# Four of sixteen transposes of the residual stream, moved from the last product into the out projection

## The chip, the core and the metric

The kernel runs on one core of a Trainium2 chip. The metric is the device time of one execution in microseconds (us). A profile is one execution recorded instruction by instruction; its span runs from the first to the last instruction and is a little shorter than the device time.

## The reference

One layer of a decoder with two attention mixers, batch 1, 256 tokens, width 1024, all in float32:

```python
h = rmsnorm(x, norm1_g)
proj = h @ w_in                      # queries, keys, values, gates
y_nsa  = nsa_attention(...)          # 8 heads, three branches
y_moba = moba_attention(...)         # 8 heads
mixed = g_nsa * (y_nsa @ w_up_nsa) + g_moba * (y_moba @ w_up_moba)
x = x + mixed @ w_out                # the out projection; this sum is x1 below
h2 = rmsnorm(x, norm2_g)
u = relu(h2 @ w_ff1)                 # 1024 -> 4096
x = x + (u * u) @ w_ff2              # 4096 -> 1024, the last product
return rmsnorm(x, norm_f_g)
```

## The kernel before

**Chunks and slots.** All weights come from memory in chunks of 128 partitions by up to 2048 numbers (1 MB), listed in `CHUNKS` in the order of use. Chunk c is loaded into a `raw` tile by SyncE (L71), split by ScalarE into a rounded high part `whi` (L87) and by VectorE into the rest `wlo` (L89), and used by TensorE. Each of the three tiles has three buffers. A product of float32 numbers is done as three matmuls: high by high, high by low, low by high (`mm3`; every one of them is recorded at the helper's line L187). The matmuls of one chunk make a slot. While slot c runs, chunk c+2 is split and chunk c+5 is loaded.

**Order inside a slot.** `run_slot` takes the list of the slot's matmuls and the events registered by `at(pos, f, ...)`. It sorts the events by `pos` and issues each of them ahead of the matmul whose place in the list, as a share of its length, reaches `pos`; so `at(0.5, ...)` in a slot of 48 matmuls comes after the first 24. Issue order is the order of every engine's own program: the schedule is written out by hand, and no planner reorders it.

**Transposed stream.** Up to the last product everything is kept with the model dimension on the partitions: `xT` (part of the tile `gx`) holds the input so, eight blocks of 128 by 256. The out projection has four slots (`for i in range(4)`, L678), each with 2 blocks of 128 model columns. Its matmuls (8 per block, three each, 48 a slot) go to `acc` tiles, and `wout_evac(i)`, issued at 0.02 of the following slot (for the last slot's first block already at 0.52 of that slot), adds the result into `x1T` (the same memory as `xT`; VectorE, L663), scales it by the second norm's gain into `h2h` (ScalarE, L666) and takes the rest `h2l` (VectorE, L669). In the slot i == 1 the attention tiles are given up and the tiles of the last stage opened in their room (`open_ff`), and near its end ScalarE issues the broadcast load of the final gain `gfb` (L687).

**The two products after it.** `ff1` has 16 slots with h2 as moving operand. `ff2` (L801) turns to token rows on the partitions: 16 chunks, each with 24 matmuls of 512 columns into four accumulators `o`, and each chunk is one slot but for the last two, which share one. The rows form of the residual, `FB["x1"]` (named x in the profile), is needed for the row norm `rstd2` in the slot i == 3 and for the last addition in `final_a`.

**The transposes.** `x1_rows` makes that form: for each pair of blocks (k2 = 0 to 3) four transposes of 128 by 128 on TensorE (L719) into one PSUM tile and one copy on ScalarE (L721) into 256 columns of `x1`. The PSUM tiles are three `acc` buffers and `yb`, the single tile that carries attention outputs before and one accumulator of the very last slot after. In the kernel before, all 16 transposes and four copies are issued at 0.5 of the slot i == 1 of `ff2`:

```python
tiles = [acc_tile(), acc_tile(), acc_tile(), ps_y.tile([128, 512], F32, name="yb")]
```

Of the kernel before, what the change touches and what calls it, by code (L numbers as in the profile page):

```python
# [8 lines left out]
F32 = mybir.dt.float32  # L9
F32R = mybir.dt.float32r  # L10
AF = mybir.ActivationFunctionType
# [29 lines left out]
def hybrid_layer(ctx: ExitStack, tc: tile.TileContext, gxd, w, w1c, small, const, gf, out):  # L41
    nc = tc.nc
    act, dve, pool, pe = nc.scalar, nc.vector, nc.gpsimd, nc.tensor
# [5 lines left out]
    ps_y = ctx.enter_context(tc.tile_pool(name="ps_y", bufs=1, space=PS))  # L49
# [6 lines left out]
    def acc_tile():  # L56
        return ps_acc.tile([128, 512], F32, name="acc")
# [35 lines left out]
    ident = cp.tile([128, 128], F32, name="ident")  # L93
# [56 lines left out]
    for k2 in range(4):  # L150
        v = xT[:, 2 * k2:2 * k2 + 2, :]
# [17 lines left out]
    def at(pos, f, *a):  # L169
        ev.append((pos, f, a))  # L170

    def run_slot(mms):
        n = len(mms)
        es = sorted(ev, key=lambda e: e[0])
        ev.clear()
        j = 0
        for i, m in enumerate(mms):
            while j < len(es) and es[j][0] <= i / n:
                es[j][1](*es[j][2])
                j += 1  # L180
            m()
        while j < len(es):
            es[j][1](*es[j][2])
            j += 1
# [24 lines left out]
    def wstat(o, c, off, nk, ncol, ah, al, ks=None, first=0, last=None):  # L209

        r = []
        last = nk - 1 if last is None else last
        for k in (range(nk) if ks is None else ks):
            a = k * ncol + off
            r += mm3(o, hi[c][:, a:a + 128], lo[c][:, a:a + 128], ah[:, k, :], al[:, k, :],
                     k == first, k == last)
        return r

    def split_events(c, hs, ls):
        for i in range(2):  # L220
            at(hs[i], split, c + 2, i, 2, "h")
        for i in range(2):
            if ls[i] <= 1:
                at(ls[i], split, c + 2, i, 2, "l")
        if ls[1] <= 1:
            at(max(ls) + 0.05, load, c + 5)

    def std_events(c):
        split_events(c, (0.0, 0.45), (0.3, 0.46))
# [394 lines left out]
    def two_blocks(c, ah, al, late=8):  # L624

        if late < 8:
            outs = [acc_tile()[:, 0:256] for _ in range(2)]
            whole = None
            order = [range(late), range(late, 8)]
        else:  # L630
            whole = acc_tile()
            outs = [whole[:, 0:256], whole[:, 256:512]]
            order = [range(8)]
        mms = []
        for ks in order:
            for m in range(2):
                mms += wstat(outs[m], c, m * 128, 8, 256, ah, al, ks=ks, last=7)
        return mms, outs, whole


    x1T = xT
    FB = {}
# [30 lines left out]
    def lo_late(pos, c):  # L673
        for k in range(2):
            at(pos, split, c + 2, k, 2, "l")
        at(pos + 0.01, load, c + 5)

    for i in range(4):  # L678
        c = C_WOUT + i
        if i == 0:  # L680
            lo_late(0.03, c - 1)
        split_events(c, (0.0, 0.1), ((0.5, 0.5), (0.3, 0.3), (0.3, 0.3), (9, 9))[i])
        for f, a in prev:
            at(0.02, f, *a)
        if i == 1:
            at(0.01, open_ff)
            at(0.9, lambda: act.dma_start(FB["gfb"], gf[None, :].to_broadcast([128, 1024])))  # L687
        if i == 3:
            outs = [acc_tile()[:, 0:256] for _ in range(2)]
            at(0.52, wout_evac, i, outs, (0,))  # L690
            run_slot([m for j in range(2)
                      for m in wstat(outs[j], c, j * 128, 8, 256, mxh, mxl)])
            prev = [(wout_evac, (i, outs, (1,)))]
        else:
            mms, outs, _ = two_blocks(c, mxh, mxl, 6 if i == 0 else 8)
            run_slot(mms)
            prev = [(wout_evac, (i, outs))]


    def ff1_evac(i, outs, whole):  # L700
# [8 lines left out]
        dve.tensor_tensor(rf, rf, rf, op=ALU.mult)  # L709
        act.activation(h, rf, AF.Copy)  # L710
        dve.tensor_tensor(l, rf, h.bitcast(F32), op=ALU.subtract)

    def x1_rows():
        tiles = [acc_tile(), acc_tile(), acc_tile(), ps_y.tile([128, 512], F32, name="yb")]
        for k2 in range(4):
            v = tiles[k2].rearrange("p (t d) -> p t d", t=2)
            for t in range(2):
                for m in range(2):
                    pe.transpose(v[:, t, m * 128:(m + 1) * 128],  # L719
                                 x1T[:, 2 * k2 + m, t * 128:(t + 1) * 128], ident)  # L720
            act.activation(FB["x1"][:, :, k2 * 256:(k2 + 1) * 256], v, AF.Copy)  # L721

    def rstd2():
        fst = FB["fst"]
# [25 lines left out]
    fst, x1, scr = FB["fst"], FB["x1"], FB["scr"]  # L750
# [3 lines left out]
    def ff2_mms(i, p):  # L754
        c = C_FF2 + i
        t, c0, n = p
        r = []
        for k in range(2):
            kt = 2 * i + k
            lh, ll = (FB[a][:, kt, t * 128:(t + 1) * 128] for a in ("sqh", "sql"))  # L760
            a = k * 1024 + c0
            r += mm3(ops[p][:, 0:n], lh, ll, hi[c][:, a:a + n], lo[c][:, a:a + n],
                     kt == (28 if p == LAST[1] else 0),
                     kt == (27 if p == PARTS[1][1] else 31))
        return r
# [35 lines left out]
    for i in range(15):  # L801
        std_events(C_FF2 + i)
        for f, a in prev:
            at(0.02, f, *a)
        prev = []
        if i == 1:
            at(0.5, x1_rows)
        if i == 3:
            at(0.1, rstd2)
        if i < 14:  # L810
            run_slot([m for p in order for m in ff2_mms(i, p)])
        else:
            ops[LAST[1]] = ps_y.tile([128, 512], F32, name="yb")
            at(0.05, first_part)
            at(0.23, final_a, PARTS[0][0], 0)
            at(0.43, final_a, PARTS[0][1], 1)
            at(0.46, final_b, 0)
            at(0.64, final_a, PARTS[1][0], 0)
            at(0.83, final_a, LAST[0], 1)
            run_slot([m for p in PARTS[0] + PARTS[1][:1] + LAST for m in ff2_mms(14, p) + ff2_mms(15, p)])  # L820
# [85 lines left out]
```

## Time and profile before

| | us |
|---|---|
| median of 3 runs | 395.99 |
| the three runs | 395.70, 395.99, 398.17 |
| device time of the profiled execution | 396.34 |
| its span | 394.5 |
| busy in it: TensorE matmul, weight load | 384.6, 346.3 |
| busy in it: VectorE, ScalarE, GpSimd | 267.5, 204.6, 9.0 |
| mean granted TensorE clock in it | 0.990 of full speed |

PE stands for TensorE's matmuls, PEld for its weight loads, DVE for VectorE, ACT for ScalarE, POOL for GpSimd and SP for SyncE. A letter q behind an engine's name is its instruction queue. A row of the timeline has start, duration, engine, line, operation and operands, and in square brackets how long the engine had been idle and what it waited for. Operand names of a matmul stand as output, then moving operand, then the operand loaded as weights. Rows of the chain view have start, length and what ran. The recorded duration of a matmul is longer than the distance to the next one, since matmuls follow one another in a pipeline; costs on TensorE are therefore read from starts.

### The profile page before, as it was taken

What the parts mean: (1) busy time and instruction counts of PE and PEld (TensorE: products, weight loads), DVE (VectorE), ACT (ScalarE), POOL (GpSimd) and SP (SyncE); (2) the same over time, 40 slices, a digit from 0 to 9 for tenths busy, and PEclk for the clock granted to TensorE, in tenths of its full rate; (3) what the DMA queues carried; (4) which work ended last, traced back from release to release, by engine and by line L of the source; (5) the groups of instructions that cost most, each with busy time, mean ns of one, the idle gap of its engine ahead of it and who ended that gap; (6) DMA issues with size and microseconds to landing.
All of it is one profiled execution on the core that took longest, in us unless ns stands there. A gap on an engine that the chain in (4) does not pass through costs nothing.

```text
span 394.5 us, 6611 instructions
## 1 busy us (share of the span) xinstructions
PE 384.6 (97%) x2687; PEld 346.3 (88%) x2687; DVE 267.5 (68%) x468; ACT 204.6 (52%) x366; POOL 9.0 (2%) x16
## 2 busy tenths in 40 slices
PE   7999999999999999999999999999999999999993
PEld 5888887778988999999999999999998888888883
DVE  5988589798778788867866665666566443444444
ACT  6474546667645555644464556455655563334412
POOL 4300000000000000000000000000000000000001
PEclk8799999999999999999999999999999999999999
DMA  7885623523323343263482655455544637555003
GB/s 240 313 339 214 213 106 114 207 89 126 108 108 107 124 157 149 108 214 106 171 311 96 226 214 185 154 197 213 185 154 195 213 130 268 169 184 208 1 2 106
DMA packets 11694, 66.34 MB, mean 168 GB/s; under 512 B 1296, under 2 KB 3600, under 8 KB 4368
## 3 DMA queue, kind: packets, MB, share of 16 engines
q1 hardware_dynamic: 11232, 65.14, 45.8%
q10 hardware_dynamic: 432, 0.79, 0.5%
q8 instruction: 21, 0.34, 0.3%
q14 instruction: 9, 0.07, 0.1%
HBM read 64.87 MB, written 1.05 MB: 167 GB/s over the span
## 4 chain that ended last, share of the span: by engine, by line
PE 93%; issue 2%; DMA 1%; DVE 1%; ACT 1%; SPq 0%; POOL 0%; POOLq 0%; DVEq 0%
PE acc L187 62%; PE o L187 21%; PE yb L187 3%; PE S L187 2%; PE tp L450 2%; PE tp L187 1%; DMA gx<-in_gx_dram 1%; PE tp L263 1%; DVE wlo L89 0%; PE acc L719 0%; POOL rstd L164 0%; PE tp L387 0%; SPq L71 0%; SPq L114 0%; DVE x L772 0%
## 5 line engine op out<-in xcount | busy, mean ns | idle before, releaser
L89 DVE TENSOR_TENSOR wlo<-raw,whi 128x1024 fp32r<-128x1024 f32 (+2 forms) x128 | 144.4, 1159 | 41.6 <-ACT whi L87 41.5
L87 ACT ACTIVATE whi<-raw 128x1024 fp32r<-128x1024 f32 (+2 forms) x128 | 124.1, 990 | 92.2 <-issue 35.5
L187 PE MATMUL acc<-h2h,whi 128*128 128x256 f32 x256 | 71.9, 281 | 0.0
L187 PE MATMUL acc<-h2l,whi 128*128 128x256 f32 x256 | 71.9, 281 | 0.0
L187 PE MATMUL acc<-h2h,wlo 128*128 128x256 f32 x256 | 71.9, 281 | 0.0
L187 PE MATMUL o<-whi,sqh 128*128 128x512 f32 (+1 forms) x128 | 49.5, 386 | 0.0
L187 PE MATMUL o<-whi,sql 128*128 128x512 f32 (+1 forms) x128 | 49.4, 386 | 0.0
L187 PE MATMUL o<-wlo,sqh 128*128 128x512 f32 (+1 forms) x128 | 49.4, 386 | 0.0
L187 PEld LDWEIGHTS acc<-h2h,whi 128*128 128x128 f32 x256 | 49.2, 192 | 0.0
L187 PEld LDWEIGHTS acc<-h2l,whi 128*128 128x128 f32 x256 | 48.0, 188 | 0.0
L187 PEld LDWEIGHTS acc<-h2h,wlo 128*128 128x128 f32 x256 | 48.0, 188 | 0.0
L187 PE MATMUL acc<-wlo,hTh 128*128 128x512 f32 (+2 forms) x96 | 38.7, 403 | 2.0 <-DVE wlo L89 1.8
L187 PE MATMUL acc<-whi,hTh 128*128 128x512 f32 (+2 forms) x96 | 38.1, 397 | 0.1
L187 PE MATMUL acc<-whi,hTl 128*128 128x512 f32 (+2 forms) x96 | 37.8, 394 | 0.0
L187 PE MATMUL acc<-hTh,whi 128*128 128x256 f32 x128 | 37.6, 293 | 0.0
L187 PE MATMUL acc<-hTl,whi 128*128 128x256 f32 x128 | 36.9, 289 | 0.0
L187 PE MATMUL acc<-hTh,wlo 128*128 128x256 f32 x128 | 36.2, 282 | 0.0
L187 PEld LDWEIGHTS o<-wlo,sqh 128*128 128x128 f32 x128 | 24.0, 188 | 4.9
L187 PEld LDWEIGHTS o<-whi,sql 128*128 128x128 f32 x128 | 24.0, 188 | 4.9
L187 PEld LDWEIGHTS o<-whi,sqh 128*128 128x128 f32 x128 | 24.0, 188 | 4.7
L187 PEld LDWEIGHTS acc<-hTh,whi 128*128 128x128 f32 x128 | 24.3, 190 | 1.4 <-issue 1.4
L187 PEld LDWEIGHTS acc<-hTl,whi 128*128 128x128 f32 x128 | 24.3, 190 | 1.0
(216 smaller groups left out, 613.5 us busy)
## 6 DMA issues: line engine op xcount, KB each, us to landing
raw<-in_ff_dram SPq DMA_DIRECT2D x32, 1024.0 KB, 4.8
raw<-in_gm_dram SPq DMA_DIRECT2D x8, 1024.0 KB, 4.8
raw<-in_wout_dram SPq DMA_DIRECT2D x4, 1024.0 KB, 4.9
raw<-in_q_dram SPq DMA_DIRECT2D x2, 1024.0 KB, 5.6
raw<-in_qm_dram SPq DMA_DIRECT2D x2, 1024.0 KB, 5.3
raw<-in_km_dram SPq DMA_DIRECT2D x2, 1024.0 KB, 4.9
raw<-in_vm_dram SPq DMA_DIRECT2D x2, 1024.0 KB, 4.8
raw<-in_upn_dram SPq DMA_DIRECT2D x2, 1024.0 KB, 4.7
```

The costliest lines, as they stand in the source:

```text
L87: act.activation(hi[c][:, a:b], raw[c][:, a:b], AF.Copy)
L89: dve.tensor_tensor(lo[c][:, a:b], raw[c][:, a:b], hi[c][:, a:b].bitcast(F32), op=ALU.subtract)
L187: pe.matmul(o, l, r, start=start, stop=stop, skip_group_check=True)
L263: pe.transpose(tp[:, j * 256 + t * 128:j * 256 + t * 128 + 128], src[:, t, (2 * i + j) * 128:(2 * i + j + 1) * 128], ident)
L450: pe.transpose(tp[:, dst:dst + 128], P[:, j, src:src + 128], ident)
```

## The change

`x1_rows` is defined earlier and takes a list of block pairs and of PSUM tiles. The pair k2 = 0 (four transposes and one copy) is issued at 0.5 of the slot i == 1 of the out projection and uses `yb`; the other three pairs stay at 0.5 of the slot i == 1 of `ff2` and use three `acc` buffers. The number of instructions and the values that they compute stay what they were.

```diff
+    def x1_rows(k2s, tiles):
+        for k2, tp in zip(k2s, tiles):
+            v = tp.rearrange("p (t d) -> p t d", t=2)
+            for t in range(2):
+                for m in range(2):
+                    pe.transpose(v[:, t, m * 128:(m + 1) * 128],
+                                 x1T[:, 2 * k2 + m, t * 128:(t + 1) * 128], ident)
+            act.activation(FB["x1"][:, :, k2 * 256:(k2 + 1) * 256], v, AF.Copy)
+
     for i in range(4):
         c = C_WOUT + i
...
         if i == 1:
             at(0.01, open_ff)
+            at(0.5, lambda: x1_rows([0], [ps_y.tile([128, 512], F32, name="yb")]))
             at(0.9, lambda: act.dma_start(FB["gfb"], gf[None, :].to_broadcast([128, 1024])))
...
-    def x1_rows():
-        tiles = [acc_tile(), acc_tile(), acc_tile(), ps_y.tile([128, 512], F32, name="yb")]
-        for k2 in range(4):
-            v = tiles[k2].rearrange("p (t d) -> p t d", t=2)
-            for t in range(2):
-                for m in range(2):
-                    pe.transpose(v[:, t, m * 128:(m + 1) * 128],
-                                 x1T[:, 2 * k2 + m, t * 128:(t + 1) * 128], ident)
-            act.activation(FB["x1"][:, :, k2 * 256:(k2 + 1) * 256], v, AF.Copy)
...
         if i == 1:
-            at(0.5, x1_rows)
+            at(0.5, x1_rows, range(1, 4), [acc_tile() for _ in range(3)])
```

## The prediction

> **What bounds the kernel now.** I began with the page: how full TensorE is, and whether its clock is held back anywhere.
>
> ```profile
> span 394.5 us, 6611 instructions
> PE 384.6 (97%) x2687; PEld 346.3 (88%) x2687; DVE 267.5 (68%) x468; ACT 204.6 (52%) x366; POOL 9.0 (2%) x16
> PEclk8799999999999999999999999999999999999999
> ```
>
> TensorE is busy for 97% of the span, and its clock is full from the third slice on. Next I asked which waits leave matmuls idle (engine, line, releaser: total us, times, longest), and what the chain of work that ended last holds from 168 us on (start, length, what).
>
> ```profile
> PE acc L187 <- DVE wlo L89: 1.8, 3, 1.0
> ...
> 98.00 0.22 PE tp L562 x2
> 122.26 0.66 PE tp L450 x6
> ...
> 168.12 131.28 PE acc L187 x1113
> 299.40 8.21 PE o L187 x36
> 307.61 1.31 PE acc L719 x12
> 308.92 0.44 PE yb L719 x4
> 309.36 73.47 PE o L187 x324
> ```
>
> The largest wait of the matmuls is 1.8 us on the first `wlo` pieces, far from the out projection and from `ff2`. From 168.12 to 382.83 the chain is TensorE alone, and the 16 transposes lie on it with 1.31 + 0.44 = 1.75 us. So a change to this stretch is worth what it adds to or takes from TensorE's own work, plus any stall that it opens. The two places in question, each as one stretch (busy us of PE, PEld, DVE, ACT, POOL; clock; DMA share; GB/s):
>
> ```profile
> 191.80:197.50 5.70, 5.70 (x51) 5.70 (x50) 5.39 (x8) 2.92 (x4) 0.00 (x0) 1.00 0.84 312
> 306.50:315.00 8.50, 8.50 (x47) 7.26 (x46) 3.65 (x4) 4.56 (x7) 0.00 (x0) 1.00 0.60 234
> ```
>
> In the old place (second row) and in the new one (first row) TensorE is busy for the whole stretch at clock 1.00. There is no hole from which the transposes leave, and none in which they would land.
>
> **The change, part by part.**
>
> *Taken out of `ff2`'s second slot: four transposes, −0.44 us.* The chain gives 1.31 us for 12, or 0.109 each, and 0.44 for the four on `yb`. Their copy on ScalarE goes too:
>
> ```profile
> 309.53 0.62 ACT L721 ACTIVATE x<-yb 128x512 f32<-128x512 f32 x1
> 312.18 2.01 ACT L87 ACTIVATE whi<-raw 128x1024 fp32r<-128x1024 f32 x2 [2.03 <-issue]
> ```
>
> ScalarE gets 0.62 us back there and has no use for it, since it idles 2.03 us behind that copy.
>
> *Put into the out projection's second slot: four transposes, +0.44 us.* There they stand between matmuls of 256 columns and interrupt the stream a second time. Whether a short group pays for going in and out is seen in the same chain: 2 transposes take 0.22, 6 take 0.66, 16 take 1.75. The line through these has no constant part: it goes from 2 to 6 with 0.110 each, and back to 0.00 at none. The one seam with 256-column matmuls that I read by starts:
>
> ```profile
> 121.98 0.28 PE L187 MATMUL acc<-hTh,wlo 128*128 128x256 f32 x1
> 122.10 0.82 PE L450 MATMUL tp<-ident,P 128*128 128x128 f32 x6
> 122.67 0.36 PE L187 MATMUL acc<-hTh,whi 128*128 128x256 f32 x1
> 122.88 0.28 PE L187 MATMUL acc<-hTl,whi 128*128 128x256 f32 x1
> ```
>
> From 121.98 to 122.88 are 0.90 us. Less two ordinary steps of 0.12 (121.98 to 122.10) this leaves 0.66 for six, again 0.110 each. I therefore cost a second group at 0.44, with 0.02 either way for reading two decimals. Removed and added cancel.
>
> *The added wait.* In the old place `x1T` has been complete for a hundred microseconds. In the new one its blocks 0 and 1 are being written by `wout_evac(0)` in the same slot, and VectorE reaches that late, since four splits stand ahead of it:
>
> ```profile
> 189.24 4.62 DVE L89 TENSOR_TENSOR wlo<-raw,whi 128x1024 fp32r<-128x1024 f32 x4
> 193.78 0.41 DVE L663 TENSOR_TENSOR gx<-gx,acc 128x256 f32<-128x256 f32 x1
> 194.12 0.41 DVE L663 TENSOR_TENSOR gx<-gx,acc 128x256 f32<-128x256 f32 x1
> 194.84 0.88 DVE L669 SCALAR_TENSOR_TENSOR h2l<-gx,h2h 128x256 fp32r<-128x256 f32 x2 [0.31 <-ACT h2h L666]
> ...
> L187 PE MATMUL acc<-mxh,whi x64: 281/281/281, 186.2 to 208.4; 128*128 128x256 f32 x64
> ...
> 194.53 0.19 PEld L187 LDWEIGHTS acc<-mxh,whi 128*128 128x128 f32 x1
> 194.65 0.28 PE L187 MATMUL acc<-mxh,whi 128*128 128x256 f32 x1
> ```
>
> The out projection's first and last high-by-high matmuls, at 186.2 and 208.4, lie 189 matmuls apart (every third of the 192 is such a one), so a step is 0.1175 and a slot of 48 takes 5.64. The second slot begins at 191.8, and its place 0.5, 24 steps on, falls at 194.65: the last row, whose weight load starts at 194.53. The transposes take over from there. The first loads block 0 as its weights; block 0 is added at 193.78 + 0.41 = 194.19, in time. The second loads block 1 about 0.11 later, at 194.64; block 1 is added at 194.12 + 0.41 = 194.53. How fast TensorE answers VectorE is shown by one of its early stalls:
>
> ```profile
> 11.27 1.39 DVE L89 TENSOR_TENSOR wlo<-raw,whi 128x384 fp32r<-128x384 f32 x1
> 12.71 0.69 PE L187 MATMUL acc<-wlo,hTh 128*128 128x384 f32 x1 [0.20 <-DVE wlo L89]
> ...
> L719 PEldq EVENT_SEMAPHORE x3: 51/51/51, 303.4 to 305.2; - x3
> ```
>
> 12.71 follows 11.27 + 1.39 = 12.66 by 0.05, so block 1 is released at about 194.58, 0.06 ahead of its use. That is a margin the size of my reading error. Against it stands the last row: in the old place the queue dealt with waits of the transposes 2 to 4 us ahead of their execution at 307.2. A queue that runs so far ahead meets the new wait early, stands at it until 194.58, and has nothing in store when it goes on. If it then needs one such 0.05 step for each of a few instructions, a bubble of 0.1 to 0.3 comes of it. Bounds: below 0.00 (a wait cannot gain), above 1.13, if the release came only with the next VectorE work, `h2l`, done at 194.84 + 0.88 = 195.72 plus 0.05, less 194.64. I take 0.05, near the lower end, because the nearest rows (ScalarE starts `h2h` at 194.29, below, 0.10 after the first addition and ahead of the end of the second) show a release per instruction. Queued behind the waiting transposes are the 24 matmuls of the slot's second half, and for them waits the next `wout_evac`.
>
> *ScalarE and its DMA queue in the new place.* The copy lands here:
>
> ```profile
> 194.29 0.51 ACT L666 ACTIVATE h2h<-gx 128x256 fp32r<-128x256 f32 x1 [1.27 <-DVE gx L663]
> 194.57 0.38 ACTq L687 DMA_DIRECT2D gfb<-in_gf_dram  x1
> 194.71 0.49 ACT L666 ACTIVATE h2h<-gx 128x256 fp32r<-128x256 f32 x1
> 195.11 1.05 ACT L87 ACTIVATE whi<-raw 128x1024 fp32r<-128x1024 f32 x1
> 197.56 1.06 ACT L87 ACTIVATE whi<-raw 128x1024 fp32r<-128x1024 f32 x1 [1.41 <-PE acc L187]
> ```
>
> The transposes end near 195.3, ScalarE is free at 195.11 + 1.05 = 196.16, and its 0.62 fits into the 1.41 of idle time before 197.56 (which itself moves to 198.0, as TensorE gives `whi` free 0.44 later). Cost nothing. Without that cover it would be 0.62 on a split that is used two slots on. The `gfb` load stands behind the copy's wait in ScalarE's queue: issued near 195.3 instead of 194.57; its first reader is `final_a` in the last slot, behind the whole of `ff1`. No instruction moves on VectorE, SyncE or GpSimd.
>
> *The sum.* −0.44 + 0.44 + 0.05 = +0.05 on the span. The profiled execution took 396.34 around its span of 394.5; the changed one would take 396.39. The median of the runs, 395.99, lies 0.35 below the profiled execution, so I expect 396.04 of the changed kernel, rounded to 396.0.
>
> A rule that speaks against the change stands in the Trainium skill's "TensorE: Matmul & The Clock Gate", "Part 4: PE-mode transpose": a transpose of 128 by 128 took about 275 ns in one kernel's context, most of it access latency. The recorded durations here agree with it in size, the distances do not: in the groups above each costs 0.11. By the page's price, paid in full for the four in the new place, an estimate is 1.10 in place of 0.44 and a time of 396.7; rival B below works that out from the rows.
>
> **The rivals.**
>
> *A, the wait decides (slower).* Place: the weight load of the second transpose in the out projection. It decides from the moment at which block 1 is released later than 194.64. Price: more than the 0.3 that the forecast still allows, up to 1.13 if the release comes with `h2l`; with the upper one 396.0 + 1.1 = 397.1. For it speaks the margin of 0.06, against it the release per instruction.
>
> *B, the small group does not overlap (slower).* Each of the four costs its recorded duration in the new place, and 0.11 still in the old:
>
> ```profile
> L719 PE MATMUL acc<-ident,gx x12: 270/272/273, 307.4 to 308.6; 128*128 128x128 f32 x12
> ```
>
> 4 × 0.272 − 0.44 = +0.65, 396.7 with the wait. This is what the transpose section of the Trainium skill's page would mean here. Against it speak the groups of 2 and 6 at 0.11 each.
>
> *C, the new place has room (faster).* If weight loads and matmuls there left a gap for the four transposes, 0.44 would be gained: 395.6. Against it: the first stretch above is full on both rows of TensorE.
>
> *D, the copy is not hidden.* ScalarE's 0.62 would reach TensorE only through a late `whi`. The split begun at 197.56, in the third slot, is for the chunk two on, the first of `ff1`, whose matmuls start behind 208.4: some 11 us lie in between, and a split half takes 1.06. Price if it did: 396.6.
>
> **How the numbers follow.** The forecast, no change but for up to 0.3 of a bubble, has 0.76; A's larger price 0.09, B 0.04, C 0.05, D 0.01; 0.05 is left for what I do not see. A difference of 1%, about 4 us, is about what a measurement of this kernel can tell from no change, as the runs alone span 395.70 to 398.17. None of the cases reaches it: A to C end between 395.6 and 397.1, so all of them count as within 1%, 0.95 with D, and the 0.05 not seen is shared out as 0.02 faster and 0.03 slower. The range goes from 395.2 (C's 395.6, less the 0.3 by which the best of the runs lies under the median) to 397.2 (A's upper price).
>
> **What would show it.** Right: in the changed profile four transposes of 0.11 near 194.65, twelve in `ff2` with 1.31, no idle time of PE charged to `gx` above 0.3, the copy between 196.1 and 196.8 ending ahead of a split that starts near 198.0, `ff2` entered 0.44 to 0.5 later than 299.4 and left for 309.36 plus 0.05. Wrong: a wait of PE on DVE gx L663 of more than 0.3 (A), the step over the group longer than 0.6 without such a wait (B), matmuls of the third slot that start no later than before (C), or a new wait of PE on `whi` (D). A time outside 395.2 to 397.2 would mean a cause that is not in this list.

## The result, and the profile after

The changed kernel takes 392.88 us (median of 4 runs, 392.15 to 393.44) against 396.99 for the kernel before in the same comparison (4 runs, 395.70 to 398.17): a ratio of 0.9896, 95% interval 0.9851 to 0.9941. That is 4 us faster where 396.0 was forecast, outside the range of 395.2 to 397.2. Two of the four runs before lie near 398; in three later comparisons the kernel before has medians of 396.24 to 396.35 (6 to 13 runs), which would make the gain some 3.4 us. The profiled execution of the changed kernel took 393.38 us, 2.96 less than the 396.34 of the one before.

The page's first lines of the changed kernel, as shown of the kernel before:

```profile
span 391.6 us, 6610 instructions
PE 380.0 (97%) x2687; PEld 342.1 (87%) x2687; DVE 267.3 (68%) x468; ACT 205.0 (52%) x366; POOL 9.1 (2%) x16
PEclk9899999999999999999999999999999999999998
```

The share of TensorE is 97% as before, the count of matmuls 2687 as before, the granted clock as full as before (1.00 between 210 and 290 us in both); but the busy time has gone from 384.6 to 380.0. The work itself has become shorter. The chain of the changed kernel says where:

```profile
168.29 0.80 PE yb L187 x8
169.09 26.70 PE acc L187 x225
195.79 0.44 PE yb L683 x4
196.23 100.66 PE acc L187 x888
296.89 8.18 PE o L187 x36
305.07 1.31 PE acc L683 x12
306.38 73.51 PE o L187 x324
```

Ahead of the four transposes (L683 here) 225 matmuls take 26.70 us, or 118.7 ns each with the first, slower steps; behind them 888 take 100.66, or 113.4 each. In the kernel before, 1113 of them took 131.28, 118.0 each, without a break from the last attention product to `ff2`. From the end of that product to the end of the last row the kernel before needs 382.83 − 168.12 = 214.71 us, the changed one 379.89 − 169.09 = 210.80: 3.91 less. Read from the starts in the steady parts, the two distances are 117.78 and 113.34 ns, and 888 × 4.44 = 3.94. So the whole gain of this stretch is in the distance of the 256-column matmuls behind the group, 768 of the 888 in `ff1`, where no line was changed. That the changed kernel enters this stretch 0.97 later (169.09 against 168.12), which takes the difference of the profiled executions down to 2.96, is the opening's doing: it comes at 167.45 to 169.53 in the other kernels below that do the same up to there.

The two distances also show in the recorded durations. First the kernel before, then the changed one, `ff1` alone (duration in ns: least, median, greatest; first and last start):

```profile
L187 PEld LDWEIGHTS acc<-h2h,whi x256: 192/192/192, 208.7 to 298.8; 128*128 128x128 f32 x128
L187 PE MATMUL acc<-h2h,whi x256: 281/281/281, 208.8 to 298.9; 128*128 128x256 f32 x128
```

```profile
L187 PEld LDWEIGHTS acc<-h2h,whi x256: 187/188/188, 209.6 to 296.3; 128*128 128x128 f32 x128
L187 PE MATMUL acc<-h2h,whi x256: 276/276/276, 209.7 to 296.4; 128*128 128x256 f32 x128
```

All 256 are alike in either kernel: 281 ns in one, 276 in the other, and the weight load that opens each group of three takes 192 or 188. The instructions, the operands and the clock are the same. I call the two distances wide (117.8) and close (113.3).

### The profile page after: what moved, and what is told of

It reads as the page before. It is cut to its first block, busy times and chain, and to the rows that moved or that the text cites. A ratio compares the mean times of both kernels' runs of the same rounds, so it can differ in the third digit from the quotient of the medians.

```text
span 391.6 us, 6610 instructions
## 1 busy us (share of the span) xinstructions
PE 380.0 (97%) x2687; PEld 342.1 (87%) x2687; DVE 267.3 (68%) x468; ACT 205.0 (52%) x366; POOL 9.1 (2%) x16
## 4 chain that ended last, share of the span: by engine, by line
PE 91%; DMA 3%; issue 2%; DVE 2%; ACT 1%; SPq 0%; POOLq 0%; POOL 0%; DVEq 0%; ACTq 0%
PE acc L187 60%; PE o L187 21%; PE yb L187 3%; PE S L187 2%; PE tp L450 2%; DMA gx<-in_gx_dram 1%; DMA raw<-in_q_dram 1%; PE tp L187 1%; PE tp L263 1%; DVE wlo L89 1%; DVE hTl L144 1%; PE acc L683 0%; PE tp L387 0%; SPq L71 0%; SPq L114 0%
## 5 line engine op out<-in xcount | busy, mean ns | idle before, releaser
L187 PE MATMUL acc<-h2h,whi 128*128 128x256 f32 x256 | 70.7, 276 | 0.0
L187 PE MATMUL acc<-h2l,whi 128*128 128x256 f32 x256 | 70.7, 276 | 0.0
L187 PE MATMUL acc<-h2h,wlo 128*128 128x256 f32 x256 | 70.7, 276 | 0.0
L187 PEld LDWEIGHTS acc<-h2h,whi 128*128 128x128 f32 x256 | 48.1, 188 | 0.0
```

The costliest lines, as they stand in the source:

```text
L187: pe.matmul(o, l, r, start=start, stop=stop, skip_group_check=True)
```

## The experiments

My theory after this comparison: the stream of 256-column matmuls can run at either distance, keeps the one it has, and four transposes put it from wide to close. The rival: something that the change really moves (less work in `ff2`'s second slot, the copy, the later `gfb` load) brings the gain.

**Only the interruption, nothing moved.**

```diff
         if i == 1:
             at(0.01, open_ff)
+            def idle_transposes():
+                yb = ps_y.tile([128, 512], F32, name="yb")
+                for k in range(4):
+                    pe.transpose(yb[:, k * 128:(k + 1) * 128], ident, ident)
+            at(0.5, idle_transposes)
```

> The kernel before with four more transposes: the identity, four times, into yb at 0.5 of the out projection's second slot; nothing reads them, and all 16 transposes of x1 and their copies stay in ff2. Theory 1 (the group itself resets the stream): the matmuls of 256 columns behind it go from 117.8 to 113.3 ns apart for the 888 up to ff2, 3.9 us gained, 0.44 paid: span 3.5 below the kernel before. Theory 2 (the gain comes from what left ff2, from the earlier copy or from the later gfb load): distance stays 117.8, span +0.44.

Measured: 393.06 us, ratio to the kernel before 0.9912 (0.988 to 0.9945). Its chain:

```profile
168.25 26.70 PE acc L187 x225
194.95 0.44 PE yb L690 x4
195.39 100.66 PE acc L187 x888
```

The same 26.70 and 100.66 as in the changed kernel, with all 16 transposes of x1 still in `ff2`. What the four compute is of no account.

**The same move to two other places.** First to 0.5 of `ff2`'s first slot, then to 0.5 of `ff1`'s ninth.

```diff
-            at(0.5, lambda: x1_rows([0], [ps_y.tile([128, 512], F32, name="yb")]))
...
+        if i == 0:      # ff2; in the second kernel: if i == 8, in ff1
+            at(0.5, lambda: x1_rows([0], [ps_y.tile([128, 512], F32, name="yb")]))
```

> The changed kernel, but the four transposes and their copy sit at 0.5 of ff2's first slot instead of the out projection's second. Theory 1: no matmul of 256 columns before ff2 is reached by the group, all stay 117.8 ns apart, the time is that of the kernel before within 0.3 us. Theory 2 (fewer transposes and copies in ff2's second slot): some 3 us faster, as in the changed kernel.

> The changed kernel, but the four transposes and their copy sit at 0.5 of the ninth slot of ff1. Theory 1: 117.8 ns up to there, 113.3 for the 24 + 7 x 48 = 360 matmuls behind, 360 x 4.43 ns = 1.6 us below the kernel before. Theory 2: 3 us, as in the changed kernel. A theory by which only the first transposes after the attention matter: no gain.

Measured: 396.22 us (0.9995, 0.9978 to 1.0013) and 394.63 us (0.9939, 0.9913 to 0.9965). The first has 1113 matmuls in 131.28 us as the kernel before. The chain of the first, then of the second:

```profile
167.90 131.28 PE acc L187 x1113
```

```profile
168.13 88.89 PE acc L187 x753
257.01 0.44 PE yb L683 x4
257.45 40.82 PE acc L187 x360
```

The second has 118.0 ns each up to the group, 113.4 behind it, and 1.6 us gained for 360 matmuls. Moving work out of `ff2`'s second slot brings nothing; the gain goes with the number of matmuls behind the group. With the first run, in which neither the copy nor the `gfb` load moved, the rival falls.

**One transpose, further ahead.** On top of the change, one transpose of the identity at 0.1 of the second up-projection slot.

```diff
+            if c == C_UPN + 1:
+                at(0.1, lambda: pe.transpose(tp_tile()[:, 0:128], ident, ident))
```

> The changed kernel with one more transpose of the identity, into a tp tile that nobody reads, at 0.1 of the second slot of the first up projection, behind the attention's last product. Theory 1: 113.3 ns already from there, for the some 220 matmuls of 256 columns between it and the group of the change: 0.98 us gained, 0.11 paid. If one transpose isn't enough, the distance there stays 117.8 and the span goes up by 0.11.

Measured: 392.02 us (0.9886, 0.9853 to 0.992); the stream is at 113.3 ns from 170.4 on, so one is enough here. Of the 0.87 us that were expected on balance only 0.21 arrived in the profile (from the end of the last attention product to the end of the last row 210.59 us, against 210.80 in the changed kernel), since the group of the change now had to wait, as it does again in a later experiment; its row in this kernel's timeline, 0.88 us long instead of 0.60:

```profile
194.22 0.88 PE L685 MATMUL yb<-ident,gx 128*128 128x128 f32 x4 [0.18 <-DVE gx L665]
```

**Must it be a transpose?** In the kernel before, at the same place, one plain float32 matmul, or one matmul of the stream's own kind with 128 columns in place of 256.

```diff
+                mm(yb[:, 0:128], ident, ident, True, True)
...
+                mm(yb[:, 0:128], hi[C_WOUT + 1][:, 0:128], mxh[:, 0, 0:128], True, True)
```

> The kernel before with one plain float32 matmul, identity by identity, 128 columns, into yb at 0.5 of the out projection's second slot; nothing reads it. If only a transpose resets the stream, the distance stays 117.8 ns and the span goes up by the matmul's own time, 0.1 to 0.3 us. If any short foreign group does, it is 113.3 ns behind it for 888 matmuls and the span 3.6 us lower.

> The kernel before with one matmul of the stream's own kind at that place (same weights, rounded operands) but with 128 columns instead of 256, into yb; nothing reads it. If a slip by one short step is enough, whatever the kind, 113.3 ns behind it and 3.8 us less. If it takes another kind of instruction or data, 117.8 ns stays and the span goes up by 0.11.

Measured, one run each: 392.37 and 392.58 us beside 395.98 for the kernel before. The chain of the second:

```profile
168.25 26.70 PE acc L187 x225
194.94 0.06 PE yb L187
195.00 100.72 PE acc L187 x888
```

Behind either the 888 matmuls are 113.3 ns apart. Half a matmul of the same kind does it: neither the transpose nor the change of number format is needed.

**Must anything be issued at all?** A first try to make TensorE stall by splitting the low parts late failed: VectorE had them ready, there was no idle moment, and the run (397.74 us, 1113 matmuls in 131.28) tells nothing on the question.

> The kernel before with no instruction more: the low parts for the ninth chunk of ff1 are split late (at 0.9 of the eighth slot), so TensorE must stall there at the head of its ninth slot by some 0.5 to 1.5 us. If an idle moment resets the stream, 113.3 ns behind it for some 380 matmuls, 1.7 us, which the stall about pays for. If it takes an instruction of another form, 117.8 ns on both sides and the span up by the stall.

The second try holds them back behind `ff1_evac`; every instruction of TensorE stays as it was:

```diff
+        elif i in (6, 7):
+            split_events(c, (0.0, 0.45), (9, 9))
...
+        if i == 7:
+            for k in range(2):
+                at(0.5, split, c + 2, k, 2, "l")
+            at(0.9, split, c + 1, 0, 2, "l")
...
+        if i == 8:
+            at(0.025, split, c, 1, 2, "l")
+            at(0.026, load, c + 3)
+            at(0.027, load, c + 4)
```

> The kernel before with the same instructions, but the second half of the low parts of ff1's ninth chunk is split only inside the ninth slot, behind ff1_evac of the slot before: TensorE must stand still there at its 15th matmul for some 1 to 3 us. If an idle moment is enough to reset the stream: 113.3 ns behind it for some 370 matmuls (1.6 us back). If it takes a matmul of another shape: 117.8 ns on both sides and the span up by the stall.

Measured, a single run: 397.83 us beside 396.26. There are two stalls where one was expected, of 1.20 and 1.73 us. Around the first, on TensorE:

```profile
253.74 0.28 PE L187 MATMUL acc<-h2h,whi 128*128 128x256 f32 x1
253.86 0.28 PE L187 MATMUL acc<-h2l,whi 128*128 128x256 f32 x1
255.35 0.39 PE L187 MATMUL acc<-h2h,wlo 128*128 128x256 f32 x1 [1.20 <-DVE wlo L89]
...
256.61 0.28 PE L187 MATMUL acc<-h2h,whi 128*128 128x256 f32 x1
256.72 0.28 PE L187 MATMUL acc<-h2l,whi 128*128 128x256 f32 x1
```

And behind the second, from the chain:

```profile
258.72 42.21 PE acc L187 x370
```

The steps are 0.12 up to the first stall and 0.11 behind it, and the 370 matmuls behind the second take 42.21 us, or 0.114 each. An idle moment without a foreign instruction took the stream from wide to close (the second left it close); here it paid for part of itself.

**Which group leaves it wide?** The stretch is wide in the kernel before from the last attention product on, a group of float32 matmuls with 64 columns of weights. Put into the changed kernel's `ff1`:

```diff
+        if i == 8:
+            def narrow_group():
+                yb = ps_y.tile([128, 512], F32, name="yb")
+                for n0 in (0, 128):
+                    for j in range(2):
+                        mm(yb[j * 64:(j + 1) * 64, n0:256], ident[:, j * 64:(j + 1) * 64],
+                           x1T[:, 0, n0:256], n0 == 0, n0 == 128)
+            at(0.5, narrow_group)
```

> The changed kernel with four float32 matmuls of the attention's last form (64 columns of weights, 256 and 128 moving columns; identity by x1's first block, into yb, nobody reads them) at 0.5 of the ninth slot of ff1. If that form is what leaves the stream slow, it goes from 113.3 back to 117.8 ns there, 360 x 4.43 ns = 1.6 us lost besides the group's own 0.8. If any interruption gives 113.3, only the 0.8 is lost.

Measured, a single run: 394.35 us; the chain:

```profile
194.59 59.86 PE acc L187 x528
254.44 0.80 PE yb L187 x8
255.25 42.60 PE acc L187 x360
```

113.4 ns ahead of it, 118.3 behind. This looked like a rule (groups with 64 columns of weights leave the stream wide, those with 128 leave it close), which the next run was to use, with one transpose in the kernel before, a single matmul behind that last attention product:

```diff
+            if c == C_UPN:
+                at(0.82, lambda: pe.transpose(tp_tile()[:, 0:128], ident, ident))
```

> The kernel before, all 16 transposes of x1 in ff2, with one transpose of the identity into a tp tile that nobody reads, behind the last attention product in the first slot of the first up projection. The rule so far (the last foreign group sets the distance until the next one; a 64-column one leaves 117.8 ns, a 128 by 128 one 113.3) gives 113.3 ns for all of the some 1110 matmuls from there to ff2: 1110 x 4.43 ns less 0.11 = 4.8 us below the kernel before, 0.9 below the changed kernel. If the rule is wrong there, no gain or only part of it.

Measured: 396.31 us, ratio 1.0003 (0.9992 to 1.0014). The chain:

```profile
168.40 0.11 PE tp L622
168.51 130.97 PE acc L187 x1112
```

The 1112 matmuls behind the transpose take 117.8 ns each, all wide. The rule fell.

**Where the moving operand lies.** The eight `gm` slots run at 120 ns, and no transpose among them changes that. `hTh` and `hTl` start 64 bytes into their room, `mxh` and `mxl` at its start.

```diff
-    hTh, hTl = act_pair("hT", 16)
+    hTh, hTl = act_pair("hT", 0)
```

> The kernel before with the tiles hTh and hTl begun 16 numbers (64 bytes) lower in their room, as mxh and mxl are. The gm slots run at about 120 ns whatever group came last. If that comes from where the moving operand lies, it goes to 113 to 118 ns there (some 380 matmuls, 0.8 to 2.5 us). If not, it stays 120, and the time too.

> The same kernel as in the run with hTh and hTl 64 bytes lower, timed. If its 389.8 us belongs to the kernel and not to that one execution: 389 to 391, 6 us below the kernel before, with 113.3 ns in the gm slots and from the last attention product to ff2.

Measured: 389.78 us in a single run, 390.66 as the median of four (0.986, 0.9842 to 0.9878). A stretch of a `gm` slot in the kernel before, then the same in this one and two rows from its later part:

```profile
131.89 3.22 PE acc L187 x27
```

```profile
130.86 3.08 PE acc L187 x27
...
165.71 0.80 PE yb L187 x8
166.51 126.36 PE acc L187 x1113
```

27 matmuls take 3.08 us instead of 3.22; the last of them are 113.3 ns apart instead of 120. And behind the last attention product, whose operands have not moved, all 1113 are now close: 126.36 instead of 131.28. In this kernel the stream came into that product at 117.8 and left it at 113.3; in the kernel before it came in at 113.4 and left at 117.8. The reverse offset, on the out projection's operands:

```diff
-    mxh, mxl = act_pair("mx", 0)
+    mxh, mxl = act_pair("mx", 16)
```

> The kernel before with mxh and mxl 64 bytes higher, as hTh and hTl lie. If the place of the moving operand sets a third distance, the out projection's 192 matmuls go from 117.8 to about 120 ns (0.4 us lost); ff1, whose operands stay, has either 117.8 or 113.3 behind it. If the place is of no account, all stay 117.8.

Measured, a single run: 393.22 us. Its high-by-high matmuls by source, and one of the later weight loads of each three (least, median, greatest ns; first and last start):

```profile
L187 PE MATMUL acc<-h2h,whi x256: 276/276/286, 209.1 to 295.9; 128*128 128x256 f32 x128
L187 PE MATMUL acc<-mxh,whi x64: 281/283/283, 186.1 to 208.8; 128*128 128x256 f32 x64
L187 PEld LDWEIGHTS acc<-mxl,whi x64: 187/192/192, 186.1 to 208.8; 128*128 128x128 f32 x64
```

The out projection runs at (208.8 − 186.1)/189 = 120.1 ns, and `ff1`, entered from there without any foreign instruction, is close. The operand's place gives a third distance, and behind the passage from it to the next operand the stream is close, where in the kernel before it stays wide over the same passage. The weight loads go with it: of the three loads of a product none takes 192 ns where the stream is close, only the first where it is wide, and all three, by their medians, at 120 ns.

**The change on a stream that is close already.** The hT offset and the change together.

> The same offset together with the change under study. If the change gains only by resetting a slow stream: the stream is already at 113.3 ns there, so moving four transposes is worth 0.0 +- 0.1 us, and the time is that of the offset alone. If four transposes are worth something in themselves in the new place: some 3 to 4 us below the offset alone. If they can also throw a fast stream back: up to 3.9 us above it.

Measured: 391.10 us (0.9869, 0.9845 to 0.9892) beside 390.66 without the change. Its chain, and then VectorE's additions and the transposes in its timeline:

```profile
192.63 0.33 PE yb L683
192.96 0.55 PE yb L683 x3
193.51 100.66 PE acc L187 x888
```

```profile
192.16 0.74 DVE L663 TENSOR_TENSOR gx<-gx,acc 128x256 f32<-128x256 f32 x2
192.63 0.88 PE L683 MATMUL yb<-ident,gx 128*128 128x128 f32 x4 [0.17 <-DVE gx L663]
```

100.66 us for 888 as in the changed kernel: nothing left to gain, and the group does not throw the stream back. It costs instead: the group takes 0.88 rather than 0.44, and the matmul before it started 0.45 ahead (192.18), so that the stretch from the end of the last attention product to the end of the last row is 210.43 us against 209.76 without the change, 0.67 more. The next step would have come at 192.29, and VectorE completes blocks 0 and 1 of `x1T` only by 192.90. The medians differ by 0.44, which is less than the spread of either kernel's runs.

**Thirty interruptions.** In the kernel before, in each of `ff1`'s slots 2 to 16 one narrow group and, later, one transpose, with places that differ modulo three.

```diff
+        if i > 0:
+            at((6 + i % 3 - 0.5) / 48, narrow_group)
+            at((27 + i // 3 % 3 - 0.5) / 48, one_transpose)
```

`narrow_group` is the one above; `one_transpose` is one transpose of the identity into `yb`.

> The kernel before, with thirty interruptions in ff1's slots 2 to 16, whose results nobody reads: in each slot one narrow float32 group (as in the narrow-group run) ahead of matmul 6, 7 or 8 and one transpose of the identity ahead of matmul 27, 28 or 29, so that all nine pairs of places within the group of three matmuls occur. Theory K (the kind of the last interruption decides): 117.8 ns behind every narrow group, 113.3 behind every transpose. Theory P (the place within the group of three decides): the distance behind an interruption goes with its place modulo 3. Theory R (it restarts the stream in either state, and neither kind nor place decides): both distances occur behind both kinds and at the same place. The span itself goes up by some 13 us of added work less what the faster stretches save.

Measured, a single run: 411.48 us beside 396.35. How one such change looks, on TensorE at the first transpose:

```profile
218.07 0.28 PE L187 MATMUL acc<-h2h,whi 128*128 128x256 f32 x1
218.18 0.28 PE L187 MATMUL acc<-h2l,whi 128*128 128x256 f32 x1
218.30 0.28 PE L187 MATMUL acc<-h2h,wlo 128*128 128x256 f32 x1
218.41 0.27 PE L747 MATMUL yb<-ident 128*128 128x128 f32 x1
...
218.99 0.28 PE L187 MATMUL acc<-h2l,whi 128*128 128x256 f32 x1
219.11 0.28 PE L187 MATMUL acc<-h2h,wlo 128*128 128x256 f32 x1
219.23 0.28 PE L187 MATMUL acc<-h2h,whi 128*128 128x256 f32 x1
```

The steps are 0.11 to 0.12 ahead (218.07 to 218.30, two steps in 0.23) and 0.12 behind (218.99 to 219.23, two in 0.24); over the whole stretches they are 113.4 and 117.7 ns, so here a transpose takes the stream from close to wide. All thirty, read over 13 to 23 steps each (every mean lies within 0.1 ns of 113.33 or 117.78; C close, W wide; matmuls of a slot are counted from 0):

| slot's i | narrow group ahead of matmul | effect | transpose ahead of matmul | effect |
|---|---|---|---|---|
| 1, 2 | 7, 8 | W to C, W to C | 27, 27 | C to W, C to W |
| 3, 4, 5 | 6, 7, 8 | W to C, W to C, W to C | 28, 28, 28 | C to W, C to W, C stays |
| 6, 7, 8 | 6, 7, 8 | C to W, C to W, W to C | 29, 29, 29 | W to C, W stays, C to W |
| 9, 10, 11 | 6, 7, 8 | W to C, C to W, C to W | 27, 27, 27 | C stays, W to C, W stays |
| 12, 13, 14 | 6, 7, 8 | W to C, W to C, W to C | 28, 28, 28 | C to W, C to W, C stays |
| 15 | 6 | C to W | 29 | W to C |

The narrow group changes the distance every time, 15 of 15, in both directions, as the last attention product does in the kernel before and in the offset one. The transpose changes it 10 times of 15, in both directions; at place 27 all four outcomes occur. Theories K and P both fall; of the three only R is left. The four slots that come twice with the same places and the same incoming distance (3 and 12, 4 and 13, 5 and 14, 6 and 15) end alike each time. And in the kernel before, the changed one and the experiments that leave the program alone up to there, 13 traces in all, the last attention product leaves the stream wide without exception. So it is not a chance event of a run.

## Why the prediction was wrong, step by step

- **The step that failed** is the premise of the sum, "a change to this stretch is worth what it adds to or takes from TensorE's own work, plus any stall that it opens". It puts at nothing any change to the step of the matmuls behind the new group, which I had read as 0.1175 in the kernel before and silently kept. The two transpose terms were right, the 0.05 for the wait was not needed, and the term that I did not have, 888 matmuls at 4.44 ns less, is −3.9 us. I treated the matmuls' distance as a property of their shape; it is also a state of the stream, and an interruption can change it.
- The trace of before held the evidence. I quoted 131.28 us for 1113 matmuls and did not set it beside a row two lines up in the same view:

```profile
163.44 3.87 PE acc L187 x34
167.32 0.80 PE yb L187 x8
```

  34 matmuls of the same shape in 3.87 us are 113.8 ns each, against 118.0 behind the narrow group. "There is no hole from which the transposes leave, and none in which they would land" was read from a busy share of 100%, and TensorE is busy all the same while its matmuls stand 4.4 ns further apart than they could.
- The terms: −0.44 and +0.44 were measured (twelve transposes in 1.31, four in 0.44 among 256-column matmuls), so rival B does not hold. The 275 ns that the Trainium skill's "TensorE: Matmul & The Clock Gate" has in "Part 4: PE-mode transpose" agree with the recorded durations of the transposes (270 to 273 ns in the kernel before), but what one adds to the stream here is 0.11 us.
- The wait: none in the changed kernel. Block 1 was added at 195.52 and the group began at 195.63, both some 0.98 later than in the forecast's rows, so the margin that I put at 0.06 was there. Rival A's mechanism is real all the same: where the stream is close, the group waits (0.88 instead of 0.44), and the change then costs 0.67 us.
- The copy was hidden as forecast, and the split behind it has 1.26 us of idle time left (of 1.41 before). The row of the changed kernel:

```profile
197.06 0.57 ACT L685 ACTIVATE x<-yb 128x512 f32<-128x512 f32 x1
198.89 1.06 ACT L87 ACTIVATE whi<-raw 128x1024 fp32r<-128x1024 f32 x1 [1.26 <-PE acc L187]
```

- Rival C had the right sign for the wrong reason: the transposes found no room, they still cost 0.44. Its price, 0.44, was a ninth of what came.
- The lower bound of the range, 395.6 less 0.3, is 395.3 and not 395.2; the measured time lies far below either. The 0.95 for "within 1%" rested on the list of causes being complete as far as 4 us go. The 0.02 for faster was all that stood for a second distance, which I had not looked for; the measured 0.9896 lies at that bound, its interval on both sides of it.

What stays open is why the stream has two distances and what decides which of them a restart takes. The runs exclude as sole cause the kind of the interruption, its place in the group of three, and the operands of the stream (one kernel has both distances on the same tiles). That the operand's place shifts the distance, and that the number of longer weight loads in each three (192 against 188 ns) goes with the distance, would fit a conflict between the reads of weights and of moving data that depends on their offset in time; this is argued, not shown.

## What to carry to other kernels

Where a long stream of equal matmuls sets the time, compute its distance (length by count, from the chain view) in every stretch and compare the stretches; equal shapes at unequal distances were worth 3.9 us here, where the matmuls' largest wait was 1.8. Try a 64-byte shift of the moving operand and one short matmul between stages, and judge by the distance behind it, since a step that seems to move work may only restart the stream. Such a gain does not belong to the moved work: with the offset alone the kernel runs at 390.66 us, below both, and the move that gained 4 us gains nothing there (by the profiles it costs 0.67).

## What the runs showed of the hardware

- In this kernel a stream of matmuls on the rounded float32 halves, with 256 moving columns and a weight load each, has two steady distances, 113.3 and 117.8 ns, at a granted clock of 1.00; either lasts for over 1100 matmuls. With the same program up to a place the distance there was the same in all 13 traces compared.
- One transpose, one half-size matmul or an idle 1.2 us switched it, and so did a change of operand from a 120 ns stretch. A group of four narrow float32 matmuls did so 15 times of 15.
- Moving operands that began 64 bytes further gave 120 ns, in the `gm` slots and in the out projection alike; in the `gm` slots the last steps of a stretch are 120 ns in spite of the interruptions before it.
